# A batched matmul kernel: where the last store is issued and awaited at the end of the program

## The chip, the cores and the metric

The kernel runs on one core of one Trainium2 chip. The metric is the device time of one execution in microseconds (us). Each call of rounds ran its versions and the kernel before on one chip; the calls were on different chips. Engine names: PE (matmul), VectorE (DVE in the views), ScalarE (ACT), GpSimd (POOL), SyncE (SP, which issues every transfer here).

## The reference

```python
batch, m, k, n = 16, 512, 512, 512      # a: [16, k, m], b: [16, k, n], float32
def reference(a, b):
    return np.matmul(a.transpose(0, 2, 1), b).astype(np.float32)
```

Inputs are 33.55 MB and the output 16.78 MB, all of which must pass the core's DMA engines once.

## The kernel before

Matrices are handled two at a time, in eight pairs. Everything stands in one hand-made section in which the author sets all semaphores. SyncE issues all loads, then all stores. VectorE casts to bfloat16, PE multiplies, ScalarE copies the sums from PSUM and raises a flag for each pair. The parts that matter here:

```python
    with tc.tile_critical(no_gpsimd_drain=True):
        for n in range(2 * pairs):
            ...                                   # loads, issued by nc.sync
        for i in range(pairs):
            nc.sync.wait_ge(s_out, i + 1)         # ScalarE's flag: pair i is in SBUF
            nc.sync.dma_start(out_v[i], o_ts[i % NO][:]).then_inc(s_o if i else s_o0, 16)
        nc.sync.wait_ge(s_o0, 16)                 # all eight stores have landed
        nc.sync.wait_ge(s_o, 16 * (pairs - 1))
        ...                                       # VectorE casts, PE matmuls (cut)
        for i in range(pairs):
            if i == NO:                           # NO = 7: the eighth pair reuses buffer o0
                nc.scalar.wait_ge(s_o0, 16)
            ...                                   # ScalarE evictions (cut)
            nc.scalar.memzero(act_done[:, i:i + 1]).then_inc(s_out, 1)
```

When such a section closes, the framework adds a handshake: SyncE sets a mark, the other engines drain and answer, SyncE collects the answers. After it come two rounds of an end barrier over all engines, with GpSimd in the middle.

## Time and profile before

| | before |
|---|---|
| timed | 124.68 us (124.62 to 124.85, 3 runs) |
| profiled run: timed, and its span | 124.76 and 122.81 us |
| first data packet | 1.96 us |
| last data packet ends | 121.05 us |
| last store complete | 121.41 us |
| its landing to the start of the end barrier's gathering | 0.705 us |
| from there to the end of the span | 0.697 us |

The two last rows are the tail, in which only sequencers (the parts of the engines that issue and wait) do anything. They meet at the instant when GpSimd has heard from the other four engines. The profile lines of this kernel stand in the prediction below.

### The profile page before, as it was taken

What the parts mean: (1) busy time and instruction counts of PE and PEld (TensorE: products, weight loads), DVE (VectorE), ACT (ScalarE), POOL (GpSimd) and SP (SyncE); (2) the same over time, 40 slices, a digit from 0 to 9 for tenths busy, and PEclk for the clock granted to TensorE, in tenths of its full rate; (3) what the DMA queues carried; (4) which work ended last, traced back from release to release, by engine and by line L of the source; (5) the groups of instructions that cost most, each with busy time, mean ns of one, the idle gap of its engine ahead of it and who ended that gap; (6) DMA issues with size and microseconds to landing.
All of it is one profiled execution on the core that took longest, in us unless ns stands there. A gap on an engine that the chain in (4) does not pass through costs nothing. (4 is left out here: it accounts for less than half of the span.)

```text
span 122.8 us, 1254 instructions
## 1 busy us (share of the span) xinstructions
PE 62.9 (51%) x512; PEld 36.0 (29%) x512; DVE 38.0 (31%) x48; ACT 31.8 (26%) x41; POOL 0.2 (0%) x4
## 2 busy tenths in 40 slices
PE   0000199989579559969919969937950000000000
PEld 0000044546256224536515536615620000000000
DVE  0021650773293091384264346328000000000000
ACT  4000000470920920290660083290092000000000
POOL 0000000000000000000000000000000000000000
PEclk9999999999999977999995899999999555555555
DMA  3999999999999999999999999999999999999991
GB/s 77 406 427 427 440 432 438 427 427 438 427 432 427 427 427 432 432 427 427 432 438 427 427 427 427 427 398 427 424 430 427 427 430 427 430 430 427 427 432 59
DMA packets 4768, 50.33 MB, mean 410 GB/s; under 512 B 416, under 2 KB 416, under 8 KB 416
## 3 DMA queue, kind: packets, MB, share of 16 engines
q1 hardware_dynamic: 4768, 50.33, 96.9%
HBM read 33.55 MB, written 16.78 MB: 410 GB/s over the span
## 5 line engine op out<-in xcount | busy, mean ns | idle before, releaser
L109 PE MATMUL ps<-bbf,abf 64*128 64x512 bf16 x512 | 62.9, 405 | 27.7 <-PEq L104 27.7
L109 PEld LDWEIGHTS ps<-bbf,abf 64*128 64x128 bf16 x512 | 36.0, 114 | 54.1 <-issue 38.1
L127 ACT COPY o<-ps 128x1024 f32<-128x1024 f32 x32 | 30.1, 1026 | 60.1 <-PE ps L109 60.1
L88 DVE CAST abf<-x 128x2048 bf16<-128x2048 f32 x16 | 19.6, 1224 | 26.8 <-PE ps L109 18.3
L88 DVE CAST bbf<-x 128x2048 bf16<-128x2048 f32 x16 | 19.6, 1224 | 20.7 <-DMA x<-in_b_dram 20.7
L132 ACT ACTIVATE act_done<-act_done 1x1 uint32<-1x1 uint32 x8 | 1.6, 197 | 0.0
L127 ACT ACT_TABLE_LOAD x1 | 1.3, 1283 | 0.9 <-SPq L62 0.9
L94 DVE MEMSET dve_done<- 1x1 f32 x16 | 0.9, 59 | 0.0
L147 POOL MEMSET const-bfloat16-1.0<- 128x1 bf16 x1 | 0.1, 102 | 0.0
L147 POOL MEMSET const-uint8-127<- 128x1 uint8 x1 | 0.1, 102 | 0.0
L147 POOL MEMSET const-float32-0.0<- 128x1 f32 x1 | 0.1, 99 | 0.2 <-issue 0.2
L147 POOL MEMSET const-float32-1.0<- 128x1 f32 x1 | 0.1, 99 | 0.0
## 6 DMA issues: line engine op xcount, KB each, us to landing
out_dram<-o SPq DMA_DIRECT2D x8, 2048.0 KB, 31.5
x<-in_a_dram SPq DMA_DIRECT2D x7, 2048.0 KB, 12.2
x<-in_b_dram SPq DMA_DIRECT2D x7, 2048.0 KB, 16.0
x<-in_a_dram SPq DMA_DIRECT2D x2, 1024.0 KB, 6.1
x<-in_b_dram SPq DMA_DIRECT2D x2, 1024.0 KB, 10.1
```

Source lines behind the costliest of these rows:

```text
L88: nc.vector.tensor_copy(out=(bbf_ts if n % 2 else abf_ts)[v][:], in_=x_ts[n % NX][:, v * RV:(v + 1) * RV, :],).then_inc(s_cast, 1)
L94: nc.vector.memset(dve_done[:, n:n + 1], 0.0).then_inc(s_in, 1)
L109: mm = nc.tensor.matmul(ps_ts[g][h][:, t % 2, :], a_m[:, t], bbf_ts[v][rows, r, :], start=(v == 0 and r == 0), stop=(v == V - 1 and r == R ...
L127: ev = nc.scalar.copy(out=o_ts[i % NO][:, g, 2 * h:2 * h + 2, :], in_=ps_ts[g][h][:])
L132: nc.scalar.memzero(act_done[:, i:i + 1]).then_inc(s_out, 1)
L147: nc = _bacc.Bacc("TRN2", target_bir_lowering=False, num_devices=1)
```

## The change

The intent is to get the closing handshake out of the tail. The first section ends ahead of the last store, so its handshake runs while stores are still streaming. The seven other stores are awaited by GpSimd in a second section, and the last store is awaited by the framework's own program end. The line `tc.no_sync_barrier()` asks the framework for no barrier ahead of the last store. The loads of the first pair stay as they were, in two halves with 8 KB runs.

```diff
-        for i in range(pairs):
+        for i in range(pairs - 1):
             nc.sync.wait_ge(s_out, i + 1)
             nc.sync.dma_start(out_v[i], o_ts[i % NO][:]).then_inc(s_o if i else s_o0, 16)
-        nc.sync.wait_ge(s_o0, 16)
-        nc.sync.wait_ge(s_o, 16 * (pairs - 1))
 ...
+    with tc.tile_critical(sync_engine=mybir.EngineType.Pool, no_gpsimd_drain=True):
+        nc.gpsimd.wait_ge(s_o0, 16)
+        nc.gpsimd.wait_ge(s_o, 16 * (pairs - 2))
+    tc.no_sync_barrier()
+    nc.sync.dma_start(out_v[pairs - 1], o_ts[(pairs - 1) % NO][:])
```

## The prediction

> **What bounds the kernel now.** I read the page from the top, to find the resource that is never idle, then the DMA view, then the waits of SyncE (the engine that issues every transfer), and last the single instructions of the final two microseconds. The page's forty slices come first:
>
> ```profile
> PE   0000199989579559969919969937950000000000
> DVE  0021650773293091384264346328000000000000
> ACT  4000000470920920290660083290092000000000
> DMA  3999999999999999999999999999999999999991
> GB/s 77 406 427 427 440 432 438 427 427 438 427 432 427 427 427 432 432 427 427 432 438 427 427 427 427 427 398 427 424 430 427 427 430 427 430 430 427 427 432 59
> ...
> q1 hardware_dynamic: 4768, 50.33, 96.9%
> ```
>
> Each digit is a busy share in tenths of a slice of 3.07 us. The DMA row is 9 in every slice but the first and the last, at about 427 GB/s. The compute rows are zero from slice 31 on: the last 30 us are nothing but stores draining. One queue, q1, carries everything and is busy 96.9% of the span. So the time is the time of 50.33 MB through the DMA engines, plus a head and a tail. No change on PE, VectorE or ScalarE can matter unless it opens a gap in that stream.
>
> How deep the queue is when the last store joins it decides what a later issue costs. The SyncE row of the waits and the stores' own line say:
>
> ```profile
> SPq L77 <- DMA out_dram<-o: 26.7, 1, 26.7
> ```
>
> ```profile
> L75 SPq DMA_DIRECT2D out_dram<-o x8: 433/1102/8533, 66.4 to 92.8; - x8
> ...
> DMA to landing us min/median/max: 20.7/31.5/37.6
> ```
>
> The eighth store is issued at 92.8 us (1.9 us of issuing, by its own record) and then SyncE does one thing: at L77 it waits 26.7 us for the stores to land. In the trace's records of landings, the stores complete at 87.07, 92.14, 97.03, 101.91, 106.79, 111.66, 116.56 and 121.41 us: one per 4.88 us, and the last 28.6 us after its issue. It joined a queue with six stores not yet landed.
>
> Then the tail. Here every instruction belongs to a sequencer and counts as not busy, so the page shows it as nothing; the listing by source line shows it:
>
> ```profile
> L77 SPq EVENT_SEMAPHORE  x1: 17/17/17, 121.4 to 121.4; - x1
> ```
>
> ```profile
> L62 SPq EVENT_SEMAPHORE  x3: 17/17/28, 121.6 to 121.9; - x3
> L62 ACTq DRAIN  x1: 8/8/8, 121.7 to 121.7; - x1
> ...
> L62 SPq NOP  x1: 13/13/13, 121.9 to 121.9; - x1
> ```
>
> ```profile
> L158 POOLq EVENT_SEMAPHORE  x4: 17/17/17, 122.1 to 122.7; - x4
> L158 SPq DRAIN  x3: 7/7/7, 122.0 to 122.3; - x3
> ```
>
> The columns are durations in ns (min/median/max), then first and last start in us. L77 is the wait for the stores. L62 is the `with` line of the hand-made section: its closing handshake. L158 is the program's own end: two rounds of all engines reporting to GpSimd and being released. To the nanosecond, the starts in the trace are: wait satisfied 121.425; branch out of the section 121.489; SyncE tells the other engines 121.644; drains of ScalarE, VectorE and PE 121.684 to 121.691; SyncE's drain 121.739; its collection of their answers 121.819, 121.872 and 121.939 (the NOP); first end drain 122.019; second 122.082. The span ends at 122.81. So the span splits into 1.96 us before the first data packet, 119.09 us of stream (to 121.05), 0.38 us until SyncE sees the last completion, **0.59 us** of closing the section (121.425 to 122.019) and 0.79 us of program end. The timed 124.68 us exceed the span by 1.87 us, which I take as constant.
>
> **What the Trainium skill says.** Three places bear on this.
> - "DMA: Bandwidth & Descriptors", section "Anatomy of one DMA": the semaphore of a DMA fires only after the last byte is confirmed landed, and DMA engines do not wait on semaphores; the issuing sequencer does. The trace agrees: last packet ends at 121.05, semaphore full at 121.41. It follows that the last landing must be awaited by someone in either kernel, and that only the sequencer's steps around it can move.
> - "Perfetto Trace Analysis", section "Per-instruction lifecycle", on sequencer-only instructions: the profile shows only the execute part; the wait before it and the propagation of the semaphore after it are hidden. The trace agrees: SyncE's seven closing instructions execute for 7 to 33 ns each, 132 ns in sum, yet they take 594 ns from first start to the next drain. I therefore cost them by distance between starts, never by duration.
> - The same page, section "Roofline" (its note on one core): the 16 DMA engines give about 435 GB/s in aggregate. The page here shows 427 to 440 in full slices, so there is no rate left to win.
>
> **The change part by part.** I read the order in which the two built programs stand, engine by engine, with their semaphores.
>
> 1. *Last store leaves the section.* In-section, SyncE issues seven stores, and its stream ends after the seventh (issue ends at 84.2 us). It then does the closing handshake, in which ScalarE answers only after its last flag write, which ends at 92.81. The new store waits for that handshake alone. In before it followed the flag directly: flag ends 92.81, store starts 92.83. After: ScalarE drain, propagation, SyncE's collecting step and its own semaphore. The distances between starts above give about 0.12 us from drain to seen (121.691 to 121.819) and 0.08 for the last step (121.939 to 122.019), so roughly 0.2 us later: issue near 93.05. The queue then holds more than 23 us of earlier stores (to 116.56). Effect on the landing: none. Same queue, shape, sixteen engines and bytes; only the completion semaphore is another.
>
> 2. *The handshake moves.* Its 0.59 us ran after the last landing; now it runs near 93 us, beside the stream. Cost on the path: 0.
>
> 3. *The wait for the seven other stores goes to GpSimd* in a second section. Its condition is full at 116.56 us. GpSimd's three waits, its mark and its two no-ops come to perhaps 0.5 us (estimate, from the similar SyncE chain), so it is done near 117.1, about 4 us ahead of the last landing. Cost on the path: 0.
>
> 4. *The final wait.* The automatic end puts it on SyncE: one wait instruction for the last store's semaphore together with GpSimd's mark (long set), then a drain, then the drain that reports to the end barrier. The first sees the landing at 121.425 as before; the next follows after the distance seen from L77 to the branch, 0.064 us, so 121.49. In before that drain began at 122.019. Saving: 122.019 - 121.489 = **0.53 us**.
>
> 5. *The end barrier* is unchanged: 0.79 us from that drain. The other four engines arrive earlier, but its round starts with the last to report, SyncE.
>
> 6. *Unchanged:* loads (the first pair still in two halves each), casts, matmuls, evictions. The head of 1.96 us stays.
>
> Sum: span 122.81 - 0.53 = 122.28; time 124.68 - 0.53 = **124.15 us**, a saving of 0.4%.
>
> **Rivals.**
> - *A wait takes the place of the one removed.* If the final wait for the last store brings its own chain of collecting steps, the saving is eaten and the time stays at 124.6 to 124.7. For it: the last landing must still be awaited, and the end adds waits on three more semaphores. Against it: all but one of those are true 4 us earlier, and the listing shows just two instructions after the landing where before had a branch, a mark, a drain and three collecting steps. I give it 1 in 8.
> - *The last store is held until the other stores land.* If it followed GpSimd's wait it would start at about 117.1. A cold queue takes 1.0 us from issue (0.94) to first packet (1.96); with 4.88 us of data and 0.36 of completion it lands near 123.3 instead of 121.4, and the time becomes 124.15 + 1.9 = 126.1 us. For it: the second section stands before the store in the text. Against it: the built program has the store waiting only for SyncE's own mark, and nothing in it ties that mark to GpSimd. Below 1 in 30.
> - *The transfers are bunched differently.* If the shift of 0.2 us at 93 us let the stream run dry, DMA share would dip there; with 28 us queued it cannot. The opposite, a gain above 0.53, would need a faster stream, and it is at its ceiling.
>
> **Range and chances.** The three timed runs before spread 124.62 to 124.85, so a median may sit 0.1 to 0.15 off; a change of chip or stream rate of 0.2% is another 0.25 us. The no-saving rival pulls the upper end. That gives 123.85 to 124.5 us. To be faster by 2% it would have to fall below 122.2, a loss of 2.5 us where the whole movable tail is 0.59; to be slower by 2%, above 127.2, more than the held-store rival makes. Hence 0.01 and 0.01, and 0.98 within 2%.
>
> **What would show each step.** The store outside the section issued near 93.05 us and landing at about 121.4 (steps 1 and 2); the slices' DMA row and rate as before; GpSimd's second section ending near 117 (step 3); on SyncE, wait to end drain in 0.06 us where it was 0.59 (step 4); 0.79 us from there to the end (step 5). A DMA dip between 116 and 119 us would mean the held store. Wrong altogether would be a time outside the span's movement: if the 1.87 us beyond the span are not constant, the profile may shorten by half a microsecond and the clock not show it.

## The result, and the profile after

The changed kernel took 124.27 us (124.20 to 124.38, 6 runs) against 124.71 us for the kernel before in the same rounds: ratio 0.9966, interval 0.9953 to 0.9979, or 0.42 us gained. The interval excludes no gain, and the change is within 2%, to which the prediction gave 0.98. The prediction said 124.15 us, 0.53 us gained.

The page of the changed kernel, the rows that answer to those in the prediction:

```profile
DMA  3999999999999999999999999999999999999993
GB/s 78 394 429 424 461 429 429 429 424 429 429 429 429 429 429 429 424 429 429 429 429 429 429 429 429 429 405 429 426 426 429 429 426 429 429 429 429 421 426 156
...
q1 hardware_dynamic: 4768, 50.33, 97.5%
```

The stream has the same number of packets and bytes. Its share of the span rose from 96.9 to 97.5%, as the span got shorter. In this profile the stream itself, first to last packet, is also 0.11 us shorter than before (118.98 against 119.09 us); in two later profiles of the changed kernel it is 119.14 and 119.15 us, so that part is scatter.

SyncE's waits (who waited on which line, for whom, us in total, times, longest):

```profile
SPq L163 <- DMA out_dram<-o: 26.4, 1, 26.4
...
SPq L62 <- PEq L62: 5.1, 1, 5.1
SPq L62 <- ACTq L62: 2.1, 1, 2.1
SPq L62 <- DVEq L62: 1.4, 1, 1.4
```

The long wait for the stores is there still, at the program's end (L163) instead of inside the section. The new rows are the closing handshake (L62) at its new place: SyncE waits 8.6 us in it for VectorE, PE and ScalarE to finish their work, and nobody misses it meanwhile. Its last step, in the stretch after 80 us:

```profile
L62 SPq NOP  x1: 13/13/13, 93.0 to 93.0; - x1
```

The store outside the section, by its own line (durations in ns, first and last start in us):

```profile
L137 SPq DMA_DIRECT2D out_dram<-o x1: 1784/1784/1784, 93.1 to 93.1; - x1
...
DMA to landing us min/median/max: 28.2/28.2/28.2
```

It is issued 0.28 us later than before (93.110 against 92.830 us) and lands at 121.32 us. Of the 0.28 us, 0.11 us is the handshake: from the end of ScalarE's flag to the issue it takes 0.138 us, where it took 0.024. The rest is that ScalarE's flag itself came later in this profile (92.972 against 92.806 us; 92.90 and 93.08 in two others of the changed kernel). GpSimd's second section, seen in the stretch after 100 us:

```profile
L133 POOLq NOP  x2: 13/13/13, 116.9 to 117.0; - x2
L133 POOLq EVENT_SEMAPHORE  x1: 17/17/17, 116.8 to 116.8; - x1
```

It is over at 117.0 us, 4.3 us ahead of the last landing. And the end of the program, after 121 us:

```profile
L163 POOLq EVENT_SEMAPHORE  x4: 17/17/17, 121.5 to 122.1; - x4
L163 SPq EVENT_SEMAPHORE  x3: 17/17/28, 121.3 to 122.2; - x3
L163 SPq DRAIN  x3: 7/7/7, 121.4 to 121.7; - x3
...
L163 POOLq EVENT_SEMAPHORE_RANGE_CLEAR  x1: 157/157/157, 121.8 to 121.8; - x1
```

SyncE sees the landing at 121.3 and its end drain starts at 121.4; no L62 row is left in this stretch. To the nanosecond: 121.340 and 121.408. In the kernel before these two were 121.425 and 122.019.

### The profile page after: what moved, and what is told of

It is laid out like the page before. It is cut to its first block, busy times and chain, and to the rows that moved or that the text cites. A ratio compares the mean times of both kernels' runs of the same rounds, so it can differ in the third digit from the quotient of the medians.

```text
span 122.2 us, 1263 instructions
## 1 busy us (share of the span) xinstructions
PE 63.2 (52%) x512; PEld 37.0 (30%) x512; DVE 38.0 (31%) x48; ACT 31.8 (26%) x41; POOL 0.2 (0%) x4
## 3 DMA queue, kind: packets, MB, share of 16 engines
q1 hardware_dynamic: 4768, 50.33, 97.5%
## 5 line engine op out<-in xcount | busy, mean ns | idle before, releaser
L107 PEld LDWEIGHTS ps<-bbf,abf 64*128 64x128 bf16 x512 | 37.0, 114 | 53.4 <-issue 37.8
```

The source lines that it names most:

```text
L107: mm = nc.tensor.matmul(ps_ts[g][h][:, t % 2, :], a_m[:, t], bbf_ts[v][rows, r, :], start=(v == 0 and r == 0), stop=(v == V - 1 and r == R ...
```

## The experiments

My theory after the result: the gain is the number of sequencer steps between the last landing and the end barrier, and nothing else. Rivals: that closing the first section early is worth something by itself; that the tail partly hides in what the timed clock doesn't see; that the place of the last store is of little account; and, since 0.42 is less than 0.53 us, that the second section costs something. The tail rows below are from each run's trace: the time from the last landing until GpSimd has gathered the four engines, and from there to the end. A version ran 4 to 6 times, the kernel before 6 or 9 times in the same rounds.

| run | timed us | before, same rounds | ratio | interval | landing to gather | gather to end |
|---|---|---|---|---|---|---|
| changed kernel | 124.27 | 124.71 | 0.9966 | 0.9953 to 0.9979 | 0.176 | 0.728 |
| after_again | 124.35 | 124.79 | 0.9963 | 0.9950 to 0.9977 | 0.177 | 0.728 |
| after_third | 124.35 | 124.73 | 0.9967 | 0.9953 to 0.9981 | 0.177 | 0.728 |
| pool_waits_all | 124.72 | 124.79 | 0.9994 | 0.9981 to 1.0008 | 0.630 | 0.706 |
| with_barrier | 124.63 | 124.79 | 0.9992 | 0.9978 to 1.0005 | 0.580 | 0.728 |
| no_second | 124.21 | 124.79 | 0.9953 | 0.9939 to 0.9966 | 0.167 | 0.705 |
| no_second_again | 124.25 | 124.73 | 0.9960 | 0.9947 to 0.9974 | 0.167 | 0.705 |
| late_store2 | 124.28 | 124.73 | 0.9962 | 0.9949 to 0.9976 | 0.176 | 0.729 |
| held_store | 126.33 | 124.67 | 1.0127 | 1.0107 to 1.0148 | 0.167 | 0.705 |
| pool_in_first | 126.02 | 124.73 | 1.0099 | 1.0083 to 1.0114 | 0.166 | 0.706 |
| more_sections_1 | 125.39 | 124.67 | 1.0053 | 1.0035 to 1.0070 | 1.312 | 0.696 |
| more_sections_4 | 127.56 | 124.67 | 1.0221 | 1.0199 to 1.0243 | 3.214 | 0.696 |

**The changed kernel again (after_again, after_third).** No edit.

> The changed kernel as it stands, in more rounds. Theory: the section's closing handshake has left the end of the span, 0.53 us by the distances between starts before, so a ratio near 0.9957 (124.15 us). Rival: only some 0.42 us of it are gained because the end of the program got longer by what the second section added, so 0.9966 again. In both, the last store's wait and the drain that reports to the end barrier are under 0.1 us apart.

> The changed kernel once more, as the partner of the next run on the same chip. In two profiles of it the landing was followed by the end barrier's start in 0.177 us and that by the end of the span in 0.728 us, 0.905 together, against 1.402 us before: 0.50 us gained, ratio 0.9960, if nothing but the tail counts.

Measured: 0.46 and 0.41 us gained (one minus the ratio, times the before time). Three sets of rounds agree on 0.41 to 0.46 us. Each interval alone is too wide to exclude 0.53, but the middle stayed below it. By the two tail columns the tail is 0.50 us shorter (1.402 to 0.904 or 0.905 us), which lies within each interval too.

**All eight stores awaited by GpSimd (pool_waits_all).**

```diff
         for i in range(pairs):
             nc.sync.wait_ge(s_out, i + 1)
             nc.sync.dma_start(...)               # all eight, in the section
-        nc.sync.wait_ge(s_o0, 16)
-        nc.sync.wait_ge(s_o, 16 * (pairs - 1))
 ...
+    with tc.tile_critical(sync_engine=mybir.EngineType.Pool, no_gpsimd_drain=True):
+        nc.gpsimd.wait_ge(s_o0, 16)
+        nc.gpsimd.wait_ge(s_o, 16 * (pairs - 1))
```

> All eight stores stay in the first section, and GpSimd's second section awaits all of them. The first section closes at 93 us as in the changed kernel, but the last landing is now followed by the second section's own closing. Theory: what counts is the chain between the last landing and the end barrier; GpSimd's steps took 0.47 us in the changed kernel, so the barrier starts about 0.56 us after the landing (0.69 before, 0.16 changed): 0.1 us gained, 124.6 us. Rival: the gain comes from closing the first section early, and then the time is that of the changed kernel, 124.27 us.

Measured: 0.9994, hardly any gain; the rival would have been 0.9966. The first section closes at 95.2 us and not at 93, since SyncE issues the eighth store in it; it is still 26 us ahead of the last landing. GpSimd's section in this run, whole span and then the program end after 121 us:

```profile
L133 POOLq NOP  x3: 13/13/13, 95.2 to 121.9; - x3
L133 POOLq EVENT_SEMAPHORE  x1: 17/17/17, 121.7 to 121.7; - x1
```

```profile
L161 SPq DRAIN  x3: 7/7/7, 121.9 to 122.3; - x3
...
L161 POOLq COMPARE_BRANCH  x1: 33/33/33, 121.6 to 121.6; - x1
```

The landing is seen at 121.5; branch 121.6, mark 121.7, answer to itself 121.8 to 121.9, and only then SyncE's drain. One closing chain has been exchanged for another of nearly the same length (0.630 against 0.705 us). Closing the first section early shows no gain by itself.

**The line that asks for no barrier (with_barrier).** The changed kernel without `tc.no_sync_barrier()`.

> The changed kernel without its line that asks for no barrier ahead of the last store. The built program then puts the store ahead of the second section, and GpSimd's second section waits for it too. Theory: the store's issue near 93.1 us and its landing stay, but GpSimd's closing follows the landing, so 124.6 us as with all eight awaited by GpSimd. Rival: the line changes nothing in time, 124.27 us.

Measured: 0.9992. The last store is issued at 93.0 us and lands at 121.50, as in the changed kernel, but GpSimd's section now waits for that landing too and closes after it (landing to gather 0.580 us). Its steps over the whole span:

```profile
L133 POOLq NOP  x3: 13/13/13, 93.0 to 121.9; - x3
L133 POOLq EVENT_SEMAPHORE  x1: 17/17/17, 121.8 to 121.8; - x1
```

In the changed kernel the same section is over at 117.0 us. So this line carries most of the gain.

**No second section (no_second, no_second_again).** The changed kernel without the second section's three lines and the no-barrier line: the seven other stores are awaited by nobody.

> The changed kernel without the second section: the seven other stores are awaited by nobody, the last one by the program's end alone[...]. Theory: the second section ends 4 us ahead of the last landing and costs nothing, so 124.27 us, equal to the changed kernel within 0.05 us. Rival: it is what holds the gain below 0.53 us, so about 124.15 us here.

> The kernel without the second section was at 0.9953 where the changed kernel was at 0.9963, 0.13 us. Its profile explains 0.033 of that (0.167 and 0.705 us of tail). Theory: the rest was scatter of the data stream, so within 0.08 us of the changed kernel in this call. Rival: the second section costs 0.1 us or more somewhere, and the distance of 0.13 us comes again.

Measured: 0.9953 and 0.9960, that is 0.59 and 0.50 us gained, against 0.46 and 0.41 for the changed kernel. So leaving the second section out seems to gain about 0.1 us, where the prediction had "cost 0". Of the two expectations this is nearer to the rival. The traces show 0.033 us of it as a shorter tail, here in the program end after 121 us:

```profile
L159 POOLq DRAIN  x2: 34/61/88, 121.7 to 122.0; - x2
...
L159 POOLq EVENT_SEMAPHORE_RANGE_CLEAR  x1: 138/138/138, 121.8 to 121.8; - x1
```

GpSimd's clearing of the semaphores takes 138 ns here against 157 in the changed kernel, and 136 in the kernel before. SyncE's wake to its end drain is 0.054 us where the changed kernel, which waits for two semaphores there, has 0.068. The two tail columns differ by 0.033 us in sum. The rest can't be pinned on the second section. In the profiles it stands mostly in the length of the stream, 119.08 and 119.00 us here against 119.14 and 119.15 in after_again and after_third; but two other profiles with a second section have 118.98 (the first of the changed kernel) and 119.00 us (late_store2, below). And late_store2, in the same call as no_second_again, has the second section and the long tail and took only 0.03 us more (124.28 against 124.25 us). So 0.033 us is shown; whether there is more, and from what, stays open.

This version has the lowest times of all that ran, and its results were correct. I would still not put it forward as it stands: it relies on the seven stores being done because a later one on the same sixteen engines is done. The Trainium skill, "DMA: Bandwidth & Descriptors", section "Queues, rings and completion order", supports that for the completion write of each engine, which lands only after the engine's earlier writes; no run here tests it beyond correct output.

**The last store held until the others have landed (held_store).**

```diff
+        nc.sync.wait_ge(s_o0, 16)                # in the first section, after seven stores
+        nc.sync.wait_ge(s_o, 16 * (pairs - 2))
 ...                                              # no second section
     nc.sync.dma_start(out_v[pairs - 1], ...)    # the last store, as in the changed kernel
```

> SyncE waits inside the first section for the seven other stores, closes it, and only then issues the last store; no second section. Theory: the store meets an empty queue; issued near 117.1 us, first packet 1.0 us later, 4.9 us of data, 0.4 us of completion, so it lands near 123.3 us and the time is about 126.1 us. Rival: the place of the store is worth little beside the handshake, under 125 us.

Measured: 126.33 us. The page shows a hole near the end of the stream:

```profile
DMA  4999999999999999999999999999999999999195
GB/s 84 392 427 445 443 427 437 427 427 421 421 421 432 437 443 427 427 432 427 427 427 421 421 421 427 437 421 424 424 424 429 427 432 432 424 424 432 76 419 216
```

The third last slice, with DMA digit 1 and 76 GB/s, is the hole: SyncE saw the seventh store at 116.56, closed the section, issued at 117.16, and the first packet moved at 118.05. The store's own line:

```profile
L135 SPq DMA_DIRECT2D out_dram<-o x1: 372/372/372, 117.2 to 117.2; - x1
...
DMA to landing us min/median/max: 6.4/6.4/6.4
```

It landed at 123.54, 2.1 us after its usual time. Its tail is as short as that of any version (0.167 us), so what the place of the store costs and what the handshake costs are here apart.

**The last store late, but with the queue not yet empty (late_store2).**

```diff
-            ...then_inc(s_o if i else s_o0, 16)
+            ...then_inc(s_o5 if i == pairs - 3 else s_o if i else s_o0, 16)
+        nc.sync.wait_ge(s_o5, 16)                # in the first section: the sixth store landed
 ...
-        nc.gpsimd.wait_ge(s_o, 16 * (pairs - 2))
+        nc.gpsimd.wait_ge(s_o, 16 * (pairs - 3))
```

A first form that counted the sixth store on the shared semaphore was refused by the race check, since two stores in flight could make up that count between them; hence the semaphore of its own.

> The late store mended: the seventh-last store but one has a semaphore of its own (sixth of eight), and SyncE stays in the first section until it has landed at 111.7 us; the last store is issued near 112.3 us with one store still queued. Theory: 19 us later than in the changed kernel and no loss, since 4.3 us of data are still queued and a store needs about 1 us from issue to first packet: the changed kernel's time of this call within 0.1 us. Rival: a shorter queue costs part of the start-up, 0.3 us or more.

Measured: 124.28 us beside 124.35 for the changed kernel. By the store's own line:

```profile
L139 SPq DMA_DIRECT2D out_dram<-o x1: 372/372/372, 112.1 to 112.1; - x1
...
DMA to landing us min/median/max: 9.3/9.3/9.3
```

Issued 19 us later than in the changed kernel, it landed at 121.37 us, as there (121.32 to 121.50). The small delay that the change gives the store is therefore free: 19 us later costs nothing, and the next run shows that 24 us later does.

**GpSimd's wait inside the first section (pool_in_first).** The plainest way to have GpSimd wait: its two lines moved into the first section, no second section.

> GpSimd's wait for the seven stores put into the first section, no second section. The built program then has SyncE collect GpSimd's answer too when it closes the section. Theory: that answer comes only after 116.5 us, so the last store is held as in the held-store run, about 126.3 us. Rival: GpSimd is not drained at the close, so the store goes at 93 us and the time is the changed kernel's.

Measured: 126.02 us. SyncE's closing handshake now includes GpSimd's answer, which came at 116.7; the store was issued at 116.82, 24 us later than in the changed kernel, and landed at 123.20. This is why a second section is needed at all if GpSimd is to await the stores.

**More closing steps after the last landing (more_sections_1, more_sections_4).** The kernel before, with this ahead of its end, once and four times:

```diff
+    for _ in range(1):                           # or 4
+        with tc.tile_critical(no_gpsimd_drain=True):
+            nc.sync.wait_ge(s_o0, 16)            # long true
```

> The kernel before, with one more section at the end that waits for nothing new: SyncE's opening and closing steps alone, after the last landing. Theory: sequencer steps after the last landing go into the time in full; some nine of them at 0.06 to 0.1 us each by the distances between starts, about 0.7 us, so 125.4 us. Rival: they overlap with what the span doesn't show, so the time stays at 124.7 us.

> The kernel before with four such sections. Theory: four times the step of one, about 2.9 us, 127.6 us, and the time beyond the span unchanged at 1.9 to 2.0 us. Rival: the first costs and the further ones hide, under 126 us.

Measured: 0.66 and 2.76 us slower (ratio minus one, times 124.67), or 0.66 and 0.69 us a section. In the traces the stretch from landing to gather grew by 0.607 and 2.509 us, 0.61 and 0.63 a section. SyncE's instructions of the four sections:

```profile
L136 SPq NOP  x8: 13/13/13, 122.1 to 124.6; - x8
L136 SPq EVENT_SEMAPHORE  x4: 17/17/17, 122.5 to 124.4; - x4
L136 SPq DRAIN  x4: 7/7/7, 122.6 to 124.5; - x4
```

Sixteen instructions of 7 to 17 ns spread over 2.5 us, and the timed clock pays for all of it: sequencer steps behind the last landing don't hide. The estimate of 0.7 us a section was a little high for the span. One part of the expectation missed: the time beyond the span was to stay at 1.9 to 2.0 us, and it was 1.97 us with one section but 2.26 with four. So some 0.3 us of the 2.76 is not in the steps that the profile shows; why is open.

## Why the prediction was right or wrong

The direction, the size class and the mechanism were right, and 124.27 us lies in the range. By its own steps:

1. *The store moves, its landing doesn't.* Right, but the closeness of the issue time (93.11 us, 93.05 predicted) is partly luck: the handshake delays the store by 0.11 us, not by the predicted 0.2, and ScalarE's flag happened to come 0.17 us later in that profile. Landing: 121.32, 121.50 and 121.50 us in three profiles, 121.41 before. This scatter of 0.18 us is not small beside the gain; the first profile's span is 0.58 us shorter than before, of which 0.085 is its early landing. That a late issue is free while enough data is queued was tested from both sides: at 112.1 us it costs nothing, at 117.2 us the landing is 2.1 us later.
2. *The handshake moves beside the stream.* Right; it runs from 84.3 to 93.0 us.
3. *The second section costs nothing on the path.* Its time was right (over at 117.0, 117.1 predicted), its cost of 0 was too low. This is the mis-sized term of the sum: 0 predicted, 0.033 us found in the tail of the traces. Without the section the kernel gains 0.59 and 0.50 us, the predicted 0.53 in the middle; with it 0.41 to 0.46, or 0.47 in late_store2. Whether it costs more than the 0.033 us is open, as said above.
4. *Saving of 0.53 us between the landing and the end drain.* Right in the trace: 0.594 us before, 0.068 us after, which is 0.526 us.
5. *The end barrier unchanged at 0.79 us.* Slightly wrong: 0.82 us, mostly GpSimd's clearing of semaphores, 157 ns instead of 136, and its drain, 88 instead of 82. Without the second section the clearing takes 138 ns, so most of this is part of the 0.033 us of step 3.
6. *The head unchanged.* Right: first packet at 1.96 to 1.98 us.

Of the rivals, the one given 1 in 8, a chain in place of the one removed, did not come true for this change, but it is what one gets without the no-barrier line. The held store did not come true either; made on purpose it takes 126.0 to 126.3 us, 126.1 predicted, and reading from the built program that the store doesn't wait for GpSimd was what ruled it out. The constant beyond the span was taken as 1.87 us from a median and a span of different runs; in the profiled runs it is 1.95 before and 1.94 to 1.97 after. It didn't matter, as it cancels. Two readings were loose: the queue that the last store joined held five earlier stores, not six (two of seven had landed by 92.83 us), and the full slices of the line shown run from 398 to 440 GB/s, not from 427. Neither touches the sum.

## What to carry to other kernels

Where a transfer queue bounds a kernel, look at what the sequencers do between the last landing and the end of the program: no busy share shows it, it is found by the distances between starts, and here each step there cost its full time. Steps that only close bookkeeping could here be moved ahead of the last transfer for nothing, as long as that transfer joined a queue that still held enough (one store, landing 4.4 us after the issue, in the latest case that cost nothing). Then check in the built program who waits for whom, for here one line decided whether the closing chain came back behind the landing.

## What the Trainium skill lacked or had wrong

- "Perfetto Trace Analysis", section "Per-instruction lifecycle": it says that waits and the propagation of a semaphore are hidden, but that page gives no durations. Here a mark of SyncE was acted on by other engines after 40 to 47 ns (121.644 to 121.684 and 121.691), by SyncE itself after 95 ns (to 121.739), and a section's opening and closing steps on SyncE took 0.61 to 0.63 us.
- "DMA: Bandwidth & Descriptors", section "Latency and other measured facts", gives about 600 ns to the first byte for this kind of DMA. Here it was 0.89 us from the start of the issue to the first packet with an idle queue (117.159 to 118.048, and 116.821 to 117.709), and 1.02 us for the first load of the program.
- The same page, section "Anatomy of one DMA", gives about 2.0 us of fixed cost, most of it the write receipt, for DMAs issued by GpSimd. A store issued by SyncE to an idle queue took 6.38 us from issue to landing in both runs; less an estimated 4.81 us for 2.10 MB at the page's 436 GB/s, that is 1.57 us, and the stretch after the last packet was 0.35 us, not most of it. No run here has a store issued by GpSimd, so this shows another path and doesn't refute the page.
- No page has what the end barrier that the framework builds into a program costs; the barriers listed are the runtime's own, around the program. From GpSimd's gathering to the end of the span it was 0.70 to 0.73 us in every run, with 136 to 158 ns of it for clearing semaphores.
